# One ordered DMA queue for x and the first weights, more engines summing squares, four residual buffers, fewer layer norm tiles and a shared last norm, in an encoder block on eight cores

## The chip, the cores and the metric

The kernel runs on all 8 cores of one Trainium2 chip, each core on its own 2,048 tokens. The metric is the device time of the slowest core, in microseconds. A program on 8 cores has a fast state and a slow one, in which the cores of a die show a lower granted clock; times of the two states are never compared here. Where one time is given for a kernel it is the median of its runs.

## The reference, cut to what matters

```python
def rms_norm(x, g):
    y = x * rsqrt(mean(x * x, axis=-1) + 1e-6)
    return y * g

# one layer; D = 1024, D_FF = 2816
u = rms_norm(h, g_mix)
z = u @ w_in                                  # value | gate | pool | gate A | gate B
gates = sigmoid(z[..., c3:] + b_gate)
y_conv = silu(layer_norm(depthwise_conv31(a_val * sigmoid(a_gate)))) @ w_conv_out
y_pool = (window_mean_minus_token(p) @ w_pool * pool_scale) @ w_pool_out
h = h + (gates_A * y_conv + gates_B * y_pool) @ w_o
v = rms_norm(h, g_ffn)
h = h + (silu(v @ w_ffn_gate) * (v @ w_ffn_up)) @ w_ffn_down
out = rms_norm(h, g_final)
```

The time goes through these stages in this order: the norm of x and the pool part of `w_in` (the start), value and gate, the convolution, the layer norm (which overlaps with the products of the folded pool weights), `w_o` with the residual, the two FFN projections, the down projection, and the last norm (the tail).

## The kernel before: the parts that the change touches

`tt`, `stt` and `act` issue one elementwise instruction on the engine named; `mm` issues a matmul; `S.dma(E, ...)` starts a transfer from engine E's queue; waits are inserted from what each instruction reads and writes.

The start. x comes in six pieces on SyncE's queue and the weights on GpSimd's queue. GpSimd issues one weight, waits for the first piece to land, and then issues the other eight.

```python
PIECES = ((0, 160), (160, 320), (480, 400), (880, 400), (1280, 400), (1680, 400))

    def x_load(p):
        o, n = PIECES[p]
        S.dma(SP, x_sem[p], xb[p]..., xp_d.ap()[:, KC * o:KC * (o + n)])
    x_load(0)
    # ... three small constants on SP
    for p in range(1, NX):
        x_load(p)
    load_one()
    S.wait_prod(POOL, x_sem[0])
    prefetch()

    def s1_squares(p):
        # ... p == 0: four squares on ACT, four on DVE, and the sums on TensorE
        for h in range(4):
            act(sq[:, 2 * h:2 * h + 2, :], x[:, 2 * h:2 * h + 2, :], AF.Square)
        tt(DVE, sq[:, 0:2, :], sq[:, 0:2, :], sq[:, 2:4, :], ALU.add)
        tt(DVE, sq[:, 4:6, :], sq[:, 4:6, :], sq[:, 6:8, :], ALU.add)
        tt(DVE, sq[:, 0:2, :], sq[:, 0:2, :], sq[:, 4:6, :], ALU.add)
        tt(DVE, sq[:, 0, :], sq[:, 0, :], sq[:, 1, :], ALU.add)

    def s1_norm(p):
        # ... matmul with ones over the squares, Ln and Exp on ACT into psum[7]
        for k in range(KC):
            stt(DVE, uT[:, k, o:o + n], xb[p][:, k, :], pcc(PC_GMIX, k), psum[7][:, 0:n], ALU.mult, ALU.mult)
```

The layer norm normalises each 512-token block in place on VectorE (`ln_steps`):

```python
        for c in range(KC):
            tt(DVE, d, d, mean[:], ALU.subtract)
            tt(DVE, d, d, rstd[:], ALU.mult)
```

The residual stage. The squares for the FFN norm go through three tiles `sq1`, GpSimd adds them up, and the log of the norm is written into `sq1[0]`, one of the three:

```python
            q = sq1[c % 3][:, 0:w_]
            act(q, src, AF.Square)
            tt(eng, a, a, q, ALU.add)             # eng is GpSimd in this stage
    def rms_stat(n, w_=TT):
        mm(psum[6][:, 0:w_], ones[:], ac1[n % 2][:, 0:w_], True, True)
        t = sq1[0][:, 0:w_]
        act(t, psum[6][:, 0:w_], AF.Ln, bias=e_rms)
        act(psum[7][:, 0:w_], t, AF.Exp, scale=-0.5)
```

The tail: the last norm has eight products on VectorE, and each is sent out from SyncE's queue.

```python
        for c in range(KC):
            x = h[:, c, o:o + w_]
            stt(DVE, x, x, pcc(PC_GFIN, c), psum[7][:, 0:w_], ALU.mult, ALU.mult)
            if w_ < TT:
                S.dma(SP, out_sem, out_d.ap()[b][...], x)
```

## Time and profile before

| | us |
|---|---|
| first three runs | 1098.68 median (1076.29 to 1101.15), two of them slow |
| the two fast runs of four | 1076.29 and 1077.07 |
| span of the slowest core in the profile (core 2) | 1074.0 |
| TensorE busy in it | 1008.9 |

Part 1 and part 2 of the page of the kernel before. Part 1 has busy time, share and instruction count of each engine; in part 2 each digit is the busy share, in tenths, of one fortieth of the span (27 us).

```profile
PE 1008.9 (94%) x5642; PEld 492.8 (46%) x5708; DVE 456.3 (42%) x710; ACT 310.1 (29%) x509; POOL 129.0 (12%) x160
PE   3788999999998999999998899999999999999996
PEclk9988999999999999999999899999999999999998
```

TensorE works all the time except for the first 110 us, a few places in the middle and the end. So whatever a change wins comes from the 65 us in which TensorE waits, and from the half-clock matmuls behind those waits. The view of waits of TensorE says for what; its columns are the total in us, how often, and the longest.

```profile
PE ps L353 <- DVE uT L374: 10.1, 13, 2.4
PE ps L353 <- DVE sqx L367: 7.9, 2, 7.4
PE ps L353 <- DMA wslot_61<-w_in: 5.4, 1, 5.4
PE ps L353 <- DMA wslot_62<-w_in: 5.1, 1, 5.1
PE ps L353 <- ACT zt_203 L364: 4.8, 1, 4.8
PE ps L353 <- DMA wslot_63<-w_in: 4.6, 1, 4.6
PE ps L353 <- DVE h1b_219 L367: 4.1, 1, 4.1
```

`uT`, `sqx` and the three weight slots belong to the start, `zt` to the layer norm stage and `h1b` to the residual stage. Why the weights are late shows in the DMA issues of the first 12 us; the last number of a row is the time from issue to landing.

```profile
xb_177<-xp SPq DMA_DIRECT2D x1, 640.0 KB, 5.6
wslot_61<-w_in POOLq DMA_DIRECT2D x1, 256.0 KB, 13.8
wslot_63<-w_in POOLq DMA_DIRECT2D x1, 256.0 KB, 24.9
```

A weight of 256 KB takes 14 to 25 us from issue to landing: it shares the DMA engines, whose busy share is 1.01 from 8 to 41 us, with x pieces of 1,280 and 1,600 KB that were issued before it. These weights are also issued late, at 7.3 us or after, because GpSimd first waits for the first piece. The end of the timeline shows the tail (start, duration, engine, what, and in brackets the idle time before it).

```profile
1065.39 0.43 DVE L367 TENSOR_TENSOR ac_0_223<-ac_0_223,sq_1_221 128x256 f32<-128x256 f32 x1 [0.73 <-ACT sq_1_221 L364]
1067.96 3.22 DVE L374 SCALAR_TENSOR_TENSOR h2b_259<-h2b_259,pc_s,ps 128x256 f32<-128x256 f32 x8 [2.14 <-ACT ps L364]
1068.51 3.82 SPq L190 DMA_DIRECT2D out<-h2b_259  x8
```

Eight products take 3.22 us and their eight issues on one queue 3.82 us; the span ends 1.7 us after the last issue.

### The profile page before, as it was taken

The numbers are of one execution on the slowest core, as the hardware profiler recorded it, in microseconds if no ns is written. First come the engines' busy times: TensorE is split into PE (matmuls) and PEld (weight loads), VectorE is DVE, ScalarE is ACT, GpSimd is POOL, SyncE is SP. The second block draws the span as 40 slices with busy tenths as digits, with TensorE's granted clock in tenths as the row PEclk, the third lists the DMA queues.
The fourth block names the chain that finished last, engine by engine and source line by source line (L and its number), as shares of the span: only waits on it lengthen the run. The fifth ranks groups of instructions, "written<-read, shape, count | busy, mean of one in ns | idle before, by whom it ended". The sixth has DMA issues, their size and how long they took to land.

```text
span 1073.3 us, 15749 instructions; the slowest of 8 cores (1070.5 to 1074.0 us)
## 1 busy us (share of the span) xinstructions
PE 1014.0 (94%) x5708; PEld 493.1 (46%) x5708; DVE 456.2 (43%) x710; ACT 310.1 (29%) x509; POOL 128.7 (12%) x160
## 2 busy tenths in 40 slices
PE   3688999999998999999998999999999999999996
PEld 2444555555443444444443344444444444444485
DVE  2344569995369532332536432122211221243454
ACT  2443333433477822212132421111111111111121
POOL 1000312241011000000063501111000000000000
PEclk9988999999999999999999899999999999999998
DMA  9600796776627011212744935656222100604112
GB/s 253 161 1 1 115 205 139 150 175 152 120 36 113 1 30 30 30 31 30 192 171 157 220 55 94 93 93 91 42 40 40 31 1 29 206 1 157 79 79 79
DMA packets 34379, 99.90 MB, mean 93 GB/s; under 512 B 4096, under 2 KB 7296, under 8 KB 31744
## 3 DMA queue, kind: packets, MB, share of 16 engines
q0 software_dynamic: 17024, 35.13, 21.3%
q1 hardware_dynamic: 17280, 63.77, 20.4%
q8 instruction: 47, 0.77, 0.3%
q14 instruction: 28, 0.23, 0.1%
HBM read 111.93 MB, written 21.04 MB: 124 GB/s over the span
## 4 chain that ended last, share of the span: by engine, by line
PE 83%; DVE 6%; DMA 5%; issue 2%; ACT 1%; POOL 1%; SPq 0%; DVEq 0%; ACTq 0%; POOLq 0%
PE ps L353 79%; PE ps L618 5%; DMA wslot_63<-w_in 2%; DVE vT L374 1%; DMA rep_186<-ad 1%; DMA rep_187<-ad 1%; DMA ad<-aT_183 1%; POOL ac_0_223 L367 1%; POOL ac_1_224 L367 0%; DVE uT L374 0%; DMA xb_177<-xp 0%; ACT ps L364 0%; DVE sqx L367 0%; DVE h2b_259 L374 0%; SPq L190 0%
## 5 line engine op out<-in xcount | busy, mean ns | idle before, releaser
L353 PE MATMUL ps<-mT,weff 128*128 128x512 bf16 x256 | 59.3, 379 | 1.5 <-DVE zt_201 L367 1.5
L353 PE MATMUL ps<-uT,wslot_60 128*128 128x512 bf16 (+4 forms) x224 | 51.1, 357 | 4.5 <-DVE uT L374 4.3
L353 PE MATMUL ps<-uT,wslot_65 128*128 128x512 bf16 (+4 forms) x216 | 47.1, 366 | 0.0
L353 PE MATMUL ps<-uT,wslot_61 128*128 128x416 bf16 (+4 forms) x192 | 40.5, 357 | 4.4 <-DMA wslot_61<-w_in 4.4
L353 PE MATMUL ps<-uT,wslot_62 128*128 128x416 bf16 (+4 forms) x192 | 39.5, 350 | 5.1 <-DMA wslot_62<-w_in 5.1
L353 PE MATMUL ps<-uT,wslot_64 128*128 128x416 bf16 (+4 forms) x192 | 41.5, 363 | 0.9 <-DVE zt_200 L367 0.9
L364 ACT ACTIVATE sgf_225<-ps 128x512 f32<-128x512 f32 x30 | 17.9, 597 | 83.3 <-PE ps L353 83.3
L353 PE MATMUL ps<-vT,wslot_67 128*128 128x512 bf16 x160 | 39.3, 381 | 1.6 <-DVE vT L374 1.4
L353 PEld LDWEIGHTS ps<-mT,weff 128*128 128x128 bf16 x256 | 25.0, 98 | 32.3 <-issue 2.5
L364 ACT ACTIVATE sgf_227<-ps 128x512 f32<-128x512 f32 x29 | 17.3, 597 | 77.4 <-PE ps L353 77.4
L364 ACT ACTIVATE sgf_226<-ps 128x512 f32<-128x512 f32 x29 | 17.3, 597 | 77.0 <-PE ps L353 77.0
L353 PE MATMUL ps<-uT,wslot_63 128*128 128x416 bf16 (+3 forms) x128 | 28.0, 346 | 12.1 <-DMA wslot_63<-w_in 5.8
L353 PE MATMUL ps<-vT,wslot_64 128*128 128x512 bf16 x160 | 38.8, 386 | 0.0
L353 PE MATMUL ps<-vT,wslot_63 128*128 128x512 bf16 x160 | 37.8, 379 | 0.0
L353 PE MATMUL ps<-vT,wslot_66 128*128 128x512 bf16 x160 | 37.8, 379 | 0.0
L353 PE MATMUL ps<-vT,wslot_61 128*128 128x512 bf16 x160 | 37.8, 379 | 0.0
L353 PE MATMUL ps<-vT,wslot_62 128*128 128x512 bf16 x160 | 37.8, 379 | 0.0
L353 PE MATMUL ps<-vT,wslot_68 128*128 128x512 bf16 x160 | 37.8, 379 | 0.0
L353 PE MATMUL ps<-vT,wslot_65 128*128 128x512 bf16 x160 | 37.8, 379 | 0.0
L353 PEld LDWEIGHTS ps<-uT,wslot_60 128*128 128x128 bf16 x224 | 21.9, 98 | 31.6 <-issue 13.2
L353 PEld LDWEIGHTS ps<-uT,wslot_65 128*128 128x128 bf16 x216 | 21.5, 101 | 22.8 <-issue 3.2
L353 PE MATMUL ps<-uT,wslot_68 128*128 128x416 bf16 (+1 forms) x144 | 30.9, 357 | 0.0
(1660 smaller groups left out, 1962.9 us busy)
## 6 DMA issues: line engine op xcount, KB each, us to landing
rep_186<-ad SPq DMA_DIRECT2D x32, 263.0 KB, 6.5
rep_187<-ad SPq DMA_DIRECT2D x32, 263.0 KB, 7.6
h1b_217<-xr SPq DMA_DIRECT2D x2, 2048.0 KB, 11.5
h1d<-h1b_217 SPq DMA_DIRECT2D x2, 2048.0 KB, 7.1
h2b_259<-h1d SPq DMA_DIRECT2D x2, 2048.0 KB, 9.4
h1b_218<-xr SPq DMA_DIRECT2D x1, 2048.0 KB, 18.9
h1b_219<-xr SPq DMA_DIRECT2D x1, 2048.0 KB, 11.0
h1d<-h1b_218 SPq DMA_DIRECT2D x1, 2048.0 KB, 15.6
```

What stands on the lines that cost most here:

```text
L353: S.op(PE, lambda e: e.matmul(out, lhsT=lhsT, rhs=rhs, start=start, stop=stop), [lhsT, rhs], [out], signal=stop if signal is None else signal)
L364: S.op(ACT, lambda e: e.activation(out=out, in_=in_, func=func, scale=scale, **kw), reads, [out])
L367: S.op(eng, lambda e: e.tensor_tensor(out=out, in0=a, in1=b, op=op), [a, b], [out])
L374: S.op(eng, lambda e: e.scalar_tensor_tensor(out=out, in0=a, scalar=s, in1=b, op0=op0, op1=op1), [a, b] + ([] if isinstance(s, float) else ...
L618: S.op(PE, lambda e, o=o, lt=lt, r_=r_, q=q, j=j: e.matmul(o, lhsT=lt, rhs=r_, start=(q == 0), stop=(q == 7), tile_position=(0, 32 * j)), ...
```

## The change

Its intent: let each weight arrive just before the matmuls that need it, take the sums of squares off VectorE at the start, free layer norm tiles, load the fourth residual block early, and share the last norm between two engines and two DMA queues. The diff, cut to its core (left out: renamings; buffer addresses; the scaling of the pool weights, which moves from VectorE to GpSimd; and three scalings by `g_final` that ScalarE does ahead of the three products on GpSimd):

```diff
-PIECES = ((0, 160), (160, 320), (480, 400), (880, 400), (1280, 400), (1680, 400))
+PIECES = ((0, 160), (160, 256), (416, 320), (736, 416), (1152, 448), (1600, 480))
@@ x and weights in one queue; the wait of GpSimd for the first piece goes
-        S.dma(SP, x_sem[p], xb[p]...)
+        S.dma(POOL, x_sem[p], xb[p]...)
-    for p in range(1, NX):
+    for p in range(NX):
         x_load(p)
-    load_one()
-    S.wait_prod(POOL, x_sem[0])
+        if p < 4:
+            load_one()
+            load_one()
     prefetch()
@@ squares: the first three pieces summed on TensorE, the others on GpSimd
-        if p == 0:
+        if p < 3:
-        tt(DVE, sq[:, 0:2, :], sq[:, 0:2, :], sq[:, 2:4, :], ALU.add)    # and three more
+        tt(POOL, sq[:, 0:2, :], sq[:, 0:2, :], sq[:, 2:4, :], ALU.add)   # and three more
@@ a new order of tiles, norms and squares; its end:
+    tiles((3,), range(4))
+    s1_squares(5)
+    s1_norm(4)
+    tiles((3,), range(4, KC))
+    tiles((4,), range(1))
+    s1_norm(5)
+    tiles((4,), range(1, KC))
+    tiles((5,), range(KC))
@@ layer norm: the last block uses no zt tiles; the folded pool weights free two more
-    zorder = list(range(NZT - 3, NZT)) + list(range(2, NZT - 3))
+    zorder = list(range(NZT - 3, NZT)) + list(range(NZT - 3))
@@ residual: four buffers, block 3 loaded at the outset
-    x_res(0)
-    x_res(1)
+    for b in (0, 1, 3):
+        x_res(b)
@@ last norm: three of eight products on GpSimd, their outputs on ScalarE's queue
+        if last:
+            rs = sgf[0][:, 0:w_]
+            act(rs, sq1[0][:, 0:w_], AF.Exp, scale=-0.5)
+        for c in (4, 0, 5, 1, 6, 2, 3, 7) if last else range(KC):
+            side = last and c in (4, 5, 6)
+            if side:
+                tt(POOL, x, x, rs, ALU.mult)
+            else:
+                stt(DVE, x, x, pcc(PC_GFIN, c), psum[7][:, 0:w_], ALU.mult, ALU.mult)
             if w_ < TT:
-                S.dma(SP, out_sem, ...)
+                S.dma(ACT if side else SP, out_sem, ...)
@@ and the last square goes straight into a second matmul with ones instead of an add
```

More of the change, by code (lines that the diff above doesn't have):

```diff
@@ L272, in build_nc @@
     weff = at("weff", [128, KC, 1024], BF16, oW)
-    xoffs = [oM, oM + 160 * 32, oM + 480 * 32, oW, oZ, oZ + 400 * 32]
+    xoffs = [oM, oM + 160 * 32, oM + 416 * 32, oZ, oZ + 416 * 32, oW]
     xb = [at(f"xb{i}", [128, KC, n], F32, o) for i, ((_, n), o) in enumerate(zip(PIECES, xoffs))]
@@ L280, in build_nc @@
     aT = [at(f"aT{i}", [128, EXT], BF16, z + i * EXT * 2) for i in range(2)]
-    wps = at("wps", [128, 4, 2, 256], BF16, z)
     z += 2 * EXT * 2
@@ L300, in build_nc @@
     h1b = [at("h1b0", [128, KC, TT], F32, oM), at("h1b1", [128, KC, TT], F32, oM + 16384),
-           at("h1b2", [128, KC, TT], F32, oZ + 16384)]
+           at("h1b2", [128, KC, TT], F32, oZ + 16384), at("h1b3", [128, KC, TT], F32, oW)]
     sq1 = [at(f"sq1_{i}", [128, TT], F32, oZ + i * 2048) for i in range(3)]
@@ L305, in build_nc @@
     vT = at("vT", [128, KC, TOK], BF16, oA)
-    foff = [oW + i * 4096 for i in range(4)] + [oM + i * 4096 for i in range(8)] + \
+    foff = [oM + i * 4096 for i in range(8)] + [oW + i * 4096 for i in range(4)] + \
            [oB + i * 4096 for i in range(10)]
@@ L344, in build_nc @@
     ad_sem = [dsem(f"d_ad{i}") for i in range(2)]
-    h1_sem = [dsem(f"d_h1{i}") for i in range(3)]
+    h1_sem = [dsem(f"d_h1{i}") for i in range(NB)]
     sp_sem = [dsem(f"d_sp{i}") for i in range(NB)]
@@ L455, in x_load @@
         o, n = PIECES[p]
-        S.dma(SP, x_sem[p], xb[p][:].rearrange("p k t -> p (k t)"), xp_d.ap()[:, KC * o:KC * (o + n)])
-    x_load(0)
+        S.dma(POOL, x_sem[p], xb[p][:].rearrange("p k t -> p (k t)"), xp_d.ap()[:, KC * o:KC * (o + n)])
     for (o, i_) in ((pc[:], pc_d.ap()), (invc[:], ic_d.ap()), (emask[:], em_d.ap())):
         S.dma(SP, cst, o, i_, val=48)
-    for p in range(1, NX):
+    for p in range(NX):
         x_load(p)
-    load_one()
-    S.wait_prod(POOL, x_sem[0])
+        if p < 4:
+            load_one()
+            load_one()
     prefetch()
@@ L484, in s1_squares @@
             act(sq[:, 2 * h:2 * h + 2, :], x[:, 2 * h:2 * h + 2, :], AF.Square)
-        tt(DVE, sq[:, 0:2, :], sq[:, 0:2, :], sq[:, 2:4, :], ALU.add)
-        tt(DVE, sq[:, 4:6, :], sq[:, 4:6, :], sq[:, 6:8, :], ALU.add)
-        tt(DVE, sq[:, 0:2, :], sq[:, 0:2, :], sq[:, 4:6, :], ALU.add)
-        tt(DVE, sq[:, 0, :], sq[:, 0, :], sq[:, 1, :], ALU.add)
+        tt(POOL, sq[:, 0:2, :], sq[:, 0:2, :], sq[:, 2:4, :], ALU.add)
+        tt(POOL, sq[:, 4:6, :], sq[:, 4:6, :], sq[:, 6:8, :], ALU.add)
+        tt(POOL, sq[:, 0:2, :], sq[:, 0:2, :], sq[:, 4:6, :], ALU.add)
+        tt(POOL, sq[:, 0, :], sq[:, 0, :], sq[:, 1, :], ALU.add)
     def s1_norm(p):
@@ L492, in s1_norm @@
         st = psum[6][:, 0:n]
-        ks = (0, 4, 1, 5, 2, 6, 3, 7) if p == 0 else (0,)
+        ks = (0, 4, 1, 5, 2, 6, 3, 7) if p < 3 else (0,)
         for i, k in enumerate(ks):
@@ L509, in pool_tile, with tiles @@
             release(f"pool{c}")
+    def tiles(ps, cs):
+        for c in cs:
+            for p in ps:
+                pool_tile(p, c)
     s1_squares(0)
@@ L513, in build_nc @@
     s1_squares(1)
-    for c in range(4):
-        pool_tile(0, c)
+    tiles((0,), (0, 1))
     s1_norm(1)
+    tiles((1,), (0, 1))
     s1_squares(2)
-    for c in range(4):
-        pool_tile(1, c)
-    for c in range(4, KC):
-        pool_tile(0, c)
-        pool_tile(1, c)
-        if c == 5:
-            s1_norm(2)
-        if c == 6:
-            s1_squares(3)
-    for p in range(2, NX):
-        for c in range(KC):
-            pool_tile(p, c)
-            if c == 2 and p + 1 < NX:
-                s1_norm(p + 1)
-            if c == 5 and p + 2 < NX:
-                s1_squares(p + 2)
+    tiles((0, 1), (2, 3))
+    s1_norm(2)
+    tiles((0, 1), (4, 5))
+    s1_squares(3)
+    tiles((2,), range(6))
+    s1_squares(4)
+    tiles((0, 1, 2), (6,))
+    s1_norm(3)
+    tiles((0, 1, 2), (7,))
+    tiles((3,), range(4))
[6 more added lines that the diff above has]
+    tiles((5,), range(KC))
     win_done = set()
@@ L707, in ln_stat @@
         mm(pq[:], ones[:], acc_q[:, tok], True, True)
-        i = ztile()
-        act(zt[i][:], pm[:], AF.Square)
         if b == NB - 1:
-            mean, rstd = pm, psum[7]
-            ids = (i,)
-        else:
-            m_ = ztile()
-            act(zt[m_][:], pm[:], AF.Copy)
-            mean, rstd = zt[m_], zt[i]
-            ids = (i, m_)
-        tt(DVE, zt[i][:], pq[:], zt[i][:], ALU.subtract)
-        lnm[b] = (mean, rstd, ids)
+            var, mean, rstd = acc_q[:, tok], pm[:], psum[7][:]
+            ids = ()
+        else:
+            ids = (ztile(), ztile())
+            var, mean = zt[ids[0]][:], zt[ids[1]][:]
+            rstd = var
+        act(var, pm[:], AF.Square)
+        if b < NB - 1:
+            act(mean, pm[:], AF.Copy)
+        tt(DVE, var, pq[:], var, ALU.subtract)
+        lnm[b] = (var, mean, rstd, ids)
     def ln_rstd(b):
-        mean, rstd, ids = lnm[b]
-        act(zt[ids[0]][:], zt[ids[0]][:], AF.Ln, bias=e_ln)
-        act(rstd[:], zt[ids[0]][:], AF.Exp, scale=-0.5)
+        var, _, rstd, _ = lnm[b]
+        act(var, var, AF.Ln, bias=e_ln)
+        act(rstd, var, AF.Exp, scale=-0.5)
     def ln_steps(b):
-        mean, rstd, ids = lnm[b]
+        _, mean, rstd, ids = lnm[b]
         out = []
@@ L731, in step @@
                 d = d_sb[c][b][:]
-                tt(DVE, d, d, mean[:], ALU.subtract)
-                tt(DVE, d, d, rstd[:], ALU.mult)
+                tt(DVE, d, d, mean, ALU.subtract)
+                tt(DVE, d, d, rstd, ALU.mult)
             out.append(step)
@@ L743, in silu, with wps @@
             act(actT[c][b][:], d_sb[c][b][:], AF.Silu, bias=pcc(PC_LNB, c), scale=pcc(PC_LNG, c))
+    def wps(g, km):
+        return slot[whome[f"wpl{g}"]][:, km * 512:km * 512 + 256]
     def wps_scale(g):
-        s_ = whome[f"wpl{g}"]
         for km in range(2):
-            src = slotf[s_][:, km * 256:(km + 1) * 256]
-            ts(DVE, wps[:, g, km, :], src, pcc(PC_PSC, 2 * g + km), ALU.mult)
+            src = slotf[whome[f"wpl{g}"]][:, km * 256:(km + 1) * 256]
+            ts(POOL, wps(g, km), src, pcc(PC_PSC, 2 * g + km), ALU.mult)
     def fold(g):
@@ L756, in fold @@
                 for km in range(2):
-                    mm(ps[:], wps[:, g, km, ki * 128:(ki + 1) * 128],
+                    mm(ps[:], wps(g, km)[:, ki * 128:(ki + 1) * 128],
                        w(f"po{2 * g + km}", None, h * 512, (h + 1) * 512), km == 0, km == 1)
@@ L793, in build_nc @@
     fold(3)
-    zfree.extend((0, 1))
     for c in range(2):
@@ L816, in x_res @@
     def x_res(b):
-        q = b % 3
-        S.dma(SP, h1_sem[q], h1b[q][:].rearrange("p k t -> p (k t)"), xr_d.ap()[b])
-    x_res(0)
-    x_res(1)
+        S.dma(SP, h1_sem[b], h1b[b][:].rearrange("p k t -> p (k t)"), xr_d.ap()[b])
+    for b in (0, 1, 3):
+        x_res(b)
     for b in range(NB):
@@ L835, in sumsq, with rms_stat @@
             tt(eng, a, a, q, ALU.add)
-    def rms_stat(n, w_=TT):
-        mm(psum[6][:, 0:w_], ones[:], ac1[n % 2][:, 0:w_], True, True)
+    def rms_stat(n, w_=TT, last=None):
+        mm(psum[6][:, 0:w_], ones[:], ac1[n % 2][:, 0:w_], True, last is None)
+        if last is not None:
+            mm(psum[6][:, 0:w_], ones[:], last, False, True)
         t = sq1[0][:, 0:w_]
@@ L843, in v_norm @@
     def v_norm(b):
-        h = h1b[b % 3]
+        h = h1b[b]
         for c in range(KC):
@@ L854, in build_nc @@
                 mm(ps[:], w(f"wo{c}", k), mrg[k][b][:], k == 0, k == KC - 1)
-            h = h1b[b % 3][:, c, :]
+            h = h1b[b][:, c, :]
             tt(DVE, h, ps[:], h, ALU.add)
@@ L862, in build_nc @@
                 v_norm(b - 1)
-                if b == 1:
-                    x_res(3)
     def gu(j, b):
@@ L903, in build_nc, with out_norm @@
         h2_load(b)
-    def out_norm(b, o, w_, n, eng):
+    def out_norm(b, o, w_, n, last=False):
         h = h2b[b % 3]
-        for c in range(KC):
+        if last:
+            rs = sgf[0][:, 0:w_]
+            act(rs, sq1[0][:, 0:w_], AF.Exp, scale=-0.5)
+        for c in (4, 0, 5, 1, 6, 2, 3, 7) if last else range(KC):
             x = h[:, c, o:o + w_]
-            stt(DVE, x, x, pcc(PC_GFIN, c), psum[7][:, 0:w_], ALU.mult, ALU.mult)
+            side = last and c in (4, 5, 6)
[3 more added lines that the diff above has]
+                stt(DVE, x, x, pcc(PC_GFIN, c), psum[7][:, 0:w_], ALU.mult, ALU.mult)
             if w_ < TT:
-                S.dma(SP, out_sem, out_d.ap()[b][:, c * TT + o:c * TT + o + w_], x)
+                S.dma(ACT if side else SP, out_sem, out_d.ap()[b][:, c * TT + o:c * TT + o + w_], x)
         if w_ == TT:
@@ L922, in build_nc @@
             tt(DVE, x, ps[:, 0:w_], x, ALU.add)
-            sumsq(x, n, c, DVE, w_)
+            if n == 4 and c == KC - 1:
+                act(sq1[c % 3][:, 0:w_], x, AF.Square)
+            else:
+                sumsq(x, n, c, DVE, w_)
+            if n == 4 and c in (4, 5, 6):
+                act(x, x, AF.Identity, scale=pcc(PC_GFIN, c))
             if c == 1 and n > 0:
@@ L926, in build_nc @@
                 rms_stat(n - 1, pw_)
-                out_norm(pb, po, pw_, n - 1, DVE)
+                out_norm(pb, po, pw_, n - 1)
                 if n == 1:
                     h2_load(3)
-    rms_stat(4, 256)
-    out_norm(3, 256, 256, 4, DVE)
+    rms_stat(4, 256, sq1[(KC - 1) % 3][:, 0:256])
+    out_norm(3, 256, 256, 4, True)
     S.wait_prod(SP, out_sem)
```

## The prediction

> **What bounds the kernel now.** TensorE: the page's first part shows it busy 1008.9 of 1074.0 us, so about 65 us of waits can go. The busy table by stretches puts them at 0 to 41 us (25 us), 51 to 97 us (8), 260 to 400 us (11), 585 to 610 us (9) and after 1064 us (9).
>
> **1. Start.** In the timeline x piece 0 lands at 6.7 us, but the second to fourth pool weights only at 21.1, 27.5 and 33.3 us: both queues share the DMA engines (share 1.01 from 8 to 41 us). TensorE waits 5.4 + 5.1 + 4.6 us for weights, then twice about 2.4 us for squares and norm (59 and 90 us), each followed by half-clock matmuls (400 columns in 0.36 us, not 0.17). Half rate after idling is in the Trainium skill, TensorE: Matmul & The Clock Gate, Part 1; the trace agrees. The first value/gate matmul starts at 115.5 us; at full clock the pool tiles need about 56 us.
>
> With one ordered queue each weight comes just before its tiles; total DMA work is unchanged (about 40 us). I walked the new order through with trace durations. The change adds 14 float32 square matmuls (about 6 us of TensorE) and GpSimd adds: at 1.27 us per 512 columns about 7 to 8.4 us a piece, against 3.66 us on VectorE (the Trainium skill, GPSIMD Engine Reference, section 3, says about twice as slow; the trace has 1.27 against 0.69 us). Data stop limiting after about 15 us; the chain square, sum, norm, uT (VectorE, 0.55 us per 400-column slice) limits then. I get value/gate starting near 96 us (88 to 104): gain **19 us**.
>
> **2. Layer norm tiles.** The 4.8 us wait for a gate tile (333 us), with 1.7 us of half clock behind it, is lack of a free tile; the change removes it. But VectorE is the chain there (44 us of norm steps from 309 us), so TensorE then waits for PSUM that VectorE has not drained. Gain **3 us**, not 8.
>
> **3. Four residual buffers.** The fourth x load (issued 571, landed 582 us) was used only at 590 us. The 4.1 us wait at 586 us is VectorE behind the FFN norm, whose log waits for GpSimd's adds (1.41 us apart) to free a square tile. The change leaves that chain. Gain **0**.
>
> **4. Last norm.** One add less (0.6 us), five VectorE products and DMA issues on one queue instead of eight (0.48 us each). Gain **1.7 us**.
>
> **Sum.** 24 us from 1076 us: **1053 us** in the fast state, 2.2% faster. Two of three runs before were in the slow state (about 1100 us), which I then expect near 1076 us. Range **1036 to 1078 us**. Chances: faster by over 2% 0.55, within 2% 0.42, slower 0.03.
>
> **What would show it.** 1: waits for pool weights gone, value/gate starting at 88 to 104 us, waits for uT and GpSimd's square sums instead. 2: the 4.8 us wait gone, longer waits for VectorE's zt products near 350 us. 3: the wait for h1b late in the residual stage still about 4 us. 4: last matmul to end 8 us, not 10.
>
> **What would make it wrong.** If the software queue moves x slower than the 290 GB/s now seen, or GpSimd's adds slow VectorE, the start gains under 10 us. If TensorE keeps full clock through the VectorE-paced tiles and norms overlap better than I walked, up to 28 us. If the residual stage's chain restarts earlier for another reason, 4 to 6 us more.

## The result, and the profile after

The kernel after took 1068.18 us (1066.94 to 1068.62, four runs, all fast); the kernel before, in the same rounds, 1087.88 us over four runs, of which two were fast (1076.29 and 1077.07). The ratio is 0.9919, with a 95% interval from 0.9895 to 0.9943: 8.7 us, where 24 us were predicted. A ratio here is the mean time of one kernel's fast runs over that of the other's of the same rounds, so it is not quite the ratio of the medians quoted.

To see where the gain came from, I took a few moments from the trace of each core and their median over the eight cores, in us from the start of the span.

| | before | after | difference |
|---|---|---|---|
| first x piece landed | 6.5 | 9.3 | +2.8 |
| first value/gate matmul (end of the start) | 114.3 | 102.0 | -12.3 |
| from there to the last convolution matmul | 177.3 | 177.0 | -0.3 |
| to the first product of the folded pool weights | 42.6 | 37.5 | -5.1 |
| to the last of those products | 182.8 | 186.5 | +3.7 |
| residual stage: first `w_o` product to first FFN matmul | 64.8 | 64.8 | 0.0 |
| first FFN matmul to last down-projection matmul | 466.4 | 466.6 | +0.2 |
| tail: from there to the end | 9.9 | 15.0 | +5.1 |

The stages sum to the result: -12.3, -1.4 for the layer norm, 0 and +5.1 make -8.6.

Part 1 of the page after, and the same rows of part 2:

```profile
PE 1012.4 (95%) x5738; PEld 497.1 (47%) x5738; DVE 438.8 (41%) x686; ACT 309.7 (29%) x513; POOL 164.5 (15%) x189
PE   4989999999998999999998899999999999999994
PEclk9989999999999999999999999999999999999998
```

The start is denser; the last slice has gone from 6 to 4 tenths. TensorE's waits after:

```profile
PE ps L352 <- DVE sqx L366: 10.9, 1, 10.9
PE ps L352 <- DVE uT L373: 7.5, 17, 1.8
PE ps L352 <- DVE h1b_218 L366: 4.1, 1, 4.1
PE ps L352 <- ACT zt_206 L363: 1.8, 1, 1.8
PE ps L352 <- DVE zt_197 L366: 1.5, 1, 1.5
PE ps L352 <- DVE zt_211 L366: 1.5, 1, 1.5
```

The three waits for weights are gone. The wait for the very first squares (`sqx`) has grown from 7.4 to 10.9 us. The 4.8 us wait for a `zt` tile has become several of about 1.5 us, most of them on VectorE. The 4.1 us wait for `h1b` is still there. The DMA issues of the first 12 us say why the first squares are late:

```profile
xb_177<-xp POOLq DMA_DIRECT2D x1, 640.0 KB, 8.6
wslot_61<-w_in POOLq DMA_DIRECT2D x1, 256.0 KB, 10.2
wslot_63<-w_in POOLq DMA_DIRECT2D x1, 256.0 KB, 15.0
```

The weights land much earlier, but the first piece of x takes 8.6 us on GpSimd's queue, where it took 5.6 us on SyncE's (these are the slowest cores; over the eight cores the medians are 7.8 and 5.4 us). It is also issued 0.5 us later, at 1.6 us instead of 1.1. Now the tail: the timeline of core 3, the slowest, then the last two stretches of its busy table (busy us and count per engine, granted clock, DMA share, GB/s), then the end of its chain of waits (start, us, engine).

```profile
1053.34 2.05 DVE L373 SCALAR_TENSOR_TENSOR h2b_259<-h2b_259,pc_s,ps 128x256 f32<-128x256 f32 x5 [2.48 <-ACT ps L363]
1053.72 2.09 POOL L366 TENSOR_TENSOR h2b_259<-h2b_259,sgf_225 128x256 f32<-128x256 f32 x3 [214.69 <-ACT sgf_225 L363]
1053.89 2.31 SPq L190 DMA_DIRECT2D out<-h2b_259  x5
1054.52 1.71 ACTq L190 DMA_DIRECT2D out<-h2b_259  x3
```

```profile
1055.00:1060.00 5.00, 0.00 (x0) 0.00 (x0) 0.39 (x1) 0.00 (x0) 0.81 (x2) 0.59 0.55 191
1060.00:1066.00 6.00, 0.00 (x0) 0.00 (x0) 0.00 (x0) 0.00 (x0) 0.00 (x0) 0.50 0.00 0
```

```profile
1053.72 0.72 POOL h2b_259 L366
1054.44 0.68 POOLq L955
1055.12 0.68 POOL h2b_259 L366
```

The norm itself went as planned: five products and three, issued by 1056.2. But the span ends at 1065.4, and in its last 5 us no engine is busy and no byte moves. The chain ends with a GpSimd product at 1055.8 us. What lies behind it is not a counted instruction. The raw records of the trace have it (start, end, sequencer, instruction; the records of core 3, most left out):

```
1055.09  1055.81  POOL   third product of the last norm
1058.15           (last output landed)
1053.76  1065.12  POOLq  DRAIN
1058.23  1058.23  SPq    DRAIN
1065.25  1065.27  POOLq  releases the closing barrier of the program
1065.30  1065.35  PEldq  leaves the barrier: end of the span
```

GpSimd's closing drain stands in its queue from 1053.76 and ends 9.3 us after GpSimd's last product, 7 us after the last output has landed, and all engines wait for it. On all eight cores it is the same 9.3 us. In the kernel before GpSimd had nothing to do after about 850 us, so its drain (852.3 to 857.3 us on core 2) lay under other work. There it ended 4.5 us after GpSimd's last instruction, the issue of a weight.

### The profile page after: what moved, and what is told of

The parts are those of the page before. It is cut to its first block, busy times and chain, and to the rows that moved or that the text cites. A ratio compares the mean times of both kernels' runs of the same rounds, so it can differ in the third digit from the quotient of the medians.

```text
span 1065.4 us, 15822 instructions; the slowest of 8 cores (1060.9 to 1065.4 us)
## 1 busy us (share of the span) xinstructions
PE 1012.4 (95%) x5738; PEld 497.1 (47%) x5738; DVE 438.8 (41%) x686; ACT 309.7 (29%) x513; POOL 164.5 (15%) x189
## 4 chain that ended last, share of the span: by engine, by line
PE 83%; DVE 7%; issue 3%; ACT 2%; POOL 2%; DMA 2%; SPq 0%; DVEq 0%; POOLq 0%; ACTq 0%
PE ps L352 79%; PE ps L625 5%; DVE uT L373 1%; DVE vT L373 1%; DMA rep_186<-ad 1%; POOL ac_1_224 L366 1%; POOL ac_0_223 L366 1%; DMA xb_177<-xp 1%; ACT ps L363 1%; ACT sqx L363 0%; ACT sq_1_221 L363 0%; ACT sq_0_220 L363 0%; ACT L363 0%; SPq L190 0%; DVEq L184 0%
## 5 line engine op out<-in xcount | busy, mean ns | idle before, releaser
L352 PE MATMUL ps<-uT,wslot_60 128*128 128x512 bf16 (+6 forms) x224 | 52.8, 354 | 10.5 <-DVE uT L373 7.5
L352 PE MATMUL ps<-uT,wslot_65 128*128 128x512 bf16 (+6 forms) x216 | 45.4, 357 | 0.0
L352 PE MATMUL ps<-uT,wslot_61 128*128 128x416 bf16 (+6 forms) x192 | 41.8, 365 | 0.0
L352 PE MATMUL ps<-uT,wslot_64 128*128 128x416 bf16 (+6 forms) x192 | 38.8, 346 | 1.3 <-DVE zt_210 L366 1.3
L352 PE MATMUL ps<-uT,wslot_62 128*128 128x416 bf16 (+6 forms) x192 | 39.3, 350 | 0.0
```

The source lines that it names most:

```text
L352: S.op(PE, lambda e: e.matmul(out, lhsT=lhsT, rhs=rhs, start=start, stop=stop), [lhsT, rhs], [out], signal=stop if signal is None else signal)
```

## The experiments

The first theory, called G in the quoted expectations, is that the tail is lost to GpSimd's closing drain, which now starts late. The main rival, Q, is that the outputs from ScalarE's DMA queue land late; any further letter is another rival, whose forecast stands in the text. For the start, the question is which part of it gave the gain and where the other 7 us of the predicted 19 went. Kernels whose name starts with a are the kernel after with one thing changed, those with b or d the kernel before with one thing changed. Stages and "drain" (from the end of GpSimd's last instruction to the end of its drain) are medians over the cores of the profiled execution. Every kernel passed the comparison with the reference.

### The tail

**a_tdve**: the last three products on VectorE, outputs still on ScalarE's queue.

```diff
-                tt(POOL, x, x, rs, ALU.mult)      # rs and its Exp go too
+                tt(DVE, x, x, psum[7][:, 0:w_], ALU.mult)
```

> After, with the three shared products of the last norm given back to VectorE (they stay on ScalarE's DMA queue). Theory G (GpSimd had work near the end, and its drain at the end of the program, 11.4 us long in the trace of after, now ends the program although all output had landed 7 us earlier): from the last down-projection matmul to the end about 8.5 us instead of 15.0, ratio to before about 0.986 (6 to 7 us below after). Rival Q (the second hardware DMA queue, ScalarE's, is what is slow to close): 15 us stays, ratio 0.992. Rival P (the prediction: sharing saves 1.7 us): giving the products back costs 0.5 to 1 us, ratio 0.993.

Measured: 1059.81 to 1061.94 us in the three fast runs (one slow run at 1203.76), ratio to before 0.9862 [0.9843, 0.9880]. From the last matmul to the end it is 8.4 us instead of 15.0. The drain still takes 9.3 us, but it begins long before the end and is hidden. G holds; Q falls, since ScalarE's queue is still in use.

**a_tsp**: all outputs on SyncE's queue, the products as in after.

```diff
-                S.dma(ACT if side else SP, out_sem, ...)
+                S.dma(SP, out_sem, ...)
```

> After, with all eight last output DMAs issued by SyncE and the three products left on GpSimd. Theory G: no change, 15 us from the last down-projection matmul to the end, ratio 0.992. Rival Q (ScalarE's DMA queue is slow to close): falls to about 9 us, ratio 0.987.

Measured: 1067.21 us, ratio 0.9920 [0.9905, 0.9936]; the tail 15.0 us, drain 9.3. The last output lands 1.7 us later than in after and the end doesn't move. Q falls a second time.

**b_pool8**: the kernel before with one tiny GpSimd add ahead of the last norm.

```diff
     rms_stat(4, 256)
+    tt(POOL, sgf[0][:, 0:8], sq1[0][:, 0:8], sq1[0][:, 0:8], ALU.add)
     out_norm(3, 256, 256, 4, DVE)
```

> Before, plus one GpSimd add of 128x8 that reads the last log, so it runs about 3.5 us after the last matmul; nothing reads its result. Theory G: GpSimd's drain ends about 9.3 us after that add whatever its size, so the program ends about 13 us after the last down-projection matmul instead of 9.9: 3 us slower, ratio 1.003. If the drain grows with the amount of GpSimd work (rival): under 1 us, ratio 1.000.

Measured: 1076.00 us, ratio 1.0003 [0.9985, 1.0021]; drain only 3.0 us, hidden under the tail of 10.0. This missed what I expected: a late GpSimd instruction alone doesn't make the long drain. Something else in the change lengthens it.

**b_tail**: the shared last norm alone, on the kernel before (the last two pieces of the diff above).

```diff
+            side = last and c in (4, 5, 6)
+            if side:
+                tt(POOL, x, x, rs, ALU.mult)
... and the rest of the shared norm, as in the change
```

> Before with the last norm's change alone (squares in the matmul, three products on GpSimd, two DMA queues), the start as before. GpSimd's drain took 3.0 us after its last instruction in before's start and 9.3 us in the new start. If the long drain belongs to the new start, the shared last norm alone gains about what was predicted: last down-projection matmul to end about 8.7 us instead of 9.9, ratio 0.999. If GpSimd's three 128x256 products make the drain long by themselves: 15.0 us, ratio 1.005.

Measured: 1075.54 us, ratio 0.9991 [0.9973, 1.0009]; tail 9.0 us against 9.9, drain 3.0. So the shared norm by itself gains about 0.9 us by the stages of the trace; in the times alone the gain is within the noise. It is a loss only together with another part of the change. Even the short drain takes part of the gain: the last output lands 8.2 us after the last matmul, and the drain ends at 8.8.

### The start

**b_start**: the start of the change alone on the kernel before (pieces, queue, squares, order).

```diff
-        S.dma(SP, x_sem[p], xb[p]...)
+        S.dma(POOL, x_sem[p], xb[p]...)
... with the new PIECES, order and GpSimd sums, as in the change
```

> Before with the start alone changed (one queue, new pieces and order, squares on TensorE and GpSimd). If the parts add: first value/gate matmul at 102 to 103 us instead of 114 to 115, 12.5 us gained, ratio 0.9885, last matmul to end unchanged at 9.9 us. That is more than after as a whole gains (0.9919), if the tail gave the difference back. The prediction put this part at 19 us: ratio 0.982.

Measured: 1063.96 us, ratio 0.9890 [0.9874, 0.9905]. The first value/gate matmul starts at 101.8 us. Its drain is 9.3 us but hidden, and its tail 9.9 us. One part of the change gains more than the whole. The layer norm stage of this kernel has the old sums, 43.0 and 182.8 us, so the two differences in that stage come from the layer norm part of the change: the fewer tiles, or the scaling of the pool weights that left VectorE with them (eight instructions of 0.35 us just before the norm steps). No run separates these two.

**a_x0sp**: the first x piece back on SyncE's queue.

```diff
-        S.dma(POOL, x_sem[p], xb[p]...)
+        S.dma(SP if p == 0 else POOL, x_sem[p], xb[p]...)
```

> After, with x piece 0 alone sent back to SyncE's hardware queue, first in it; pieces 1 to 5 and the weights stay in GpSimd's queue. If the missing part of the start is the late landing of piece 0 (9.3 us, median of the cores, against 6.5 before): it lands near 6.5 us and the first value/gate matmul moves from 102.0 to about 99 us, ratio 0.989. If the later chain (square, sum, norm, uT) sets the end of the stage by itself: under 1 us.

Measured: 1064.85 us, ratio 0.9897 [0.9882, 0.9911]. The piece lands at 6.3 us instead of 9.3 and value/gate starts at 99.7 us, 2.3 us earlier than in after. Most of the late landing of the first piece is on the critical path.

**a_swap**: the norm of piece 4 ahead of the squares of piece 5.

```diff
     tiles((3,), range(4))
-    s1_squares(5)
     s1_norm(4)
+    s1_squares(5)
     tiles((3,), range(4, KC))
-    tiles((4,), range(1))
+    tiles((4,), range(4))
     s1_norm(5)
-    tiles((4,), range(1, KC))
+    tiles((4,), range(4, KC))
```

The fourth tile instead of the first before the norm of piece 5 is part of the edit too. It was built for what the timeline of the kernel after shows on ScalarE and VectorE between 66 and 76 us:

```profile
66.52 3.67 ACT L363 ACTIVATE sqx<-xb_182 128x960 f32<-128x960 f32 x4
70.09 0.59 ACT L363 ACTIVATE ps<-ps,eps_s 128x448 f32<-128x448 f32 x1
71.47 4.82 DVE L373 SCALAR_TENSOR_TENSOR uT<-xb_181,pc_s,ps 128x448 bf16<-128x448 f32 x8 [11.28 <-ACT ps L363]
```

The statistics of piece 4 are ready at 66.8 us, but its log waits 3.3 us behind the squares of piece 5; VectorE stands idle for 11 us, and TensorE is then paced by the `uT` slices. The matmuls of 448 columns after that take 0.28 us, and 2 us later 0.21 (eight in 2.22 and in 1.68 us); the granted clock in the busy table is 0.50 from 76.9 to 78.6 us, 0.73 over the first of these groups and 1.00 after it. Half rate after idling is what the Trainium skill has in "TensorE: Matmul & The Clock Gate", Part 1; here the trace shows a granted clock of 0.50, and half mixed with full rate over this group of eight.

> After, with the norm of piece 4 put before the squares of piece 5 in program order, and the norm of piece 5 after the fourth tile of piece 4. In after ScalarE does the squares of piece 5 (3.7 us) before the log of piece 4, so uT of piece 4 comes late, TensorE is paced by it for 4 us and drops to half clock. If that is what the start lacks: first value/gate matmul 4 us earlier (98 us), ratio 0.988. If GpSimd's adds (8.1 us for piece 5) limit: under 1 us, or later.

Measured: 1061.80 and 1061.91 us in the two fast runs (two slow ones at 1091 and 1251), ratio 0.9866 [0.9846, 0.9886]. Value/gate starts at 97.7 us, 4.3 us earlier.

**a_dveadd**: the sums of squares back on VectorE, in the new order.

```diff
-        tt(POOL, sq[:, 0:2, :], sq[:, 0:2, :], sq[:, 2:4, :], ALU.add)   # all four adds
+        tt(DVE, sq[:, 0:2, :], sq[:, 0:2, :], sq[:, 2:4, :], ALU.add)
```

> After, with the sums of squares of pieces 3 to 5 on VectorE again instead of GpSimd. Prediction's reading (GpSimd's slow adds limit the start): first value/gate matmul 3 to 5 us earlier. Reading from the trace of after (the adds are done before TensorE asks for them): within 1 us of 102. For GpSimd's drain at the end (9.3 us after its last instruction in all kernels with the new start, 3.0 us in before with one small add): if the float32 adds of the start make it long, 3 us, and 8.5 to 9.5 us from last matmul to end; if the x loads on GpSimd's queue do, 9.3 us and 15.0 us.

Measured: only one of five runs was fast, 1071.04 us, so there is no ratio. In its profile value/gate starts at 105.5 us, 3.5 us later than in after. So GpSimd's slow sums (7.2 to 8.1 us a piece) seem to help: with them TensorE waits 7.5 us for `uT`, without them 9.3, which fits with VectorE having 3.8 to 4.3 us of adds a piece less ahead of `uT`. Drain still 9.3 us: those sums aren't what lengthens it.

**a_xsp**: all x pieces back on SyncE's queue, the rest as in after. GpSimd issues its weights at once, without the old wait for the first piece.

```diff
-        S.dma(POOL, x_sem[p], xb[p]...)
+        S.dma(SP, x_sem[p], xb[p]...)
```

> After, with all six x loads on SyncE's queue (the weights, in the same order, stay alone in GpSimd's), everything else as in after. If the x loads on GpSimd's queue make its drain long: drain 3.0 us, last matmul to end about 9 us instead of 15.0. If the burst of instructions or something else of the new start does: 9.3 and 15.0. For the start: if the single ordered queue is what brings its gain, the pool weights come late again and the first value/gate matmul goes back to 108 us or later; if the new pieces and order do, it stays within 2 us of 102.

Measured: 1062.74 us, ratio 0.9859 [0.9844, 0.9875]. Value/gate starts at 103.8 us, only 1.8 us later than with the single queue, while the tail falls to 8.7 us with a drain of 3.0. In this kernel the single ordered queue is worth 1.8 us at the start and costs 6.3 us at the end. One reason shows in the landings (medians of the cores): the second to fourth weights land at 12.2, 16.8 and 22.6 us here, 12.5, 17.4 and 18.7 in after, and 20.3, 26.5 and 32.8 in before. So they are early with x on SyncE's queue as well; there too GpSimd no longer waits for the first piece before it issues them.

### What lengthens the drain

**d_x5pool**: before, with the tiny add and the last x piece on GpSimd's queue. **d_xall**: the same with all six pieces there, in the old order of issue (all x first, and GpSimd still waits for the first piece).

```diff
-        S.dma(SP, x_sem[p], xb[p]...)
+        S.dma(POOL if p == 5 else SP, x_sem[p], xb[p]...)      # d_x5pool
+        S.dma(POOL, x_sem[p], xb[p]...)                         # d_xall
```

> Before with the 128x8 GpSimd add near the end (as in b_pool8) and one of the six x loads, piece 5, issued from GpSimd's queue (first in it, so the start is disturbed; only the drain is read). If x loads on that queue make the drain long: 9.3 us after the add instead of 3.0, or a sixth of the way (about 4 us) if each load adds its share. If only the whole burst of 15 DMAs does it, or something else of the new start: 3.0 us.

> Before with the 128x8 GpSimd add near the end and all six x loads on GpSimd's queue, in before's pieces and order (the start is disturbed; only the drain is read). If the loads together make it long: 9.3 us after the add, so the program ends about 16 us after the last down-projection matmul. Else 3.0 us and 10.

Measured: drain 3.0 us in both (1078.3 us, and 1085.59 us with value/gate as late as 122.1 us, because the weights then land behind all of x). x loads on that queue are not enough.

**a_oldpieces**: after, with the piece sizes of before. **a_wait1**: after, with GpSimd waiting for piece 1 before it issues piece 3, so that fewer transfers are outstanding.

```diff
-PIECES = ((0, 160), (160, 256), (416, 320), (736, 416), (1152, 448), (1600, 480))
+PIECES = ((0, 160), (160, 320), (480, 400), (880, 400), (1280, 400), (1680, 400))     # a_oldpieces
@@
     for p in range(NX):
+        if p == 3:
+            S.wait_prod(POOL, x_sem[1])                                                # a_wait1
         x_load(p)
```

> The kernel after with the piece sizes of the kernel before (160, 320, four of 400 columns), everything else as after: x on GpSimd's queue between the weights, the new order of compute. One look, for the length of GpSimd's closing drain and the end. If the drain is long because of the larger x pieces (up to 480 columns, rows of 15,360 bytes against 12,800), it is 3.0 us here and the end is about 9 us after the last down-projection product. If it is long because x and weights alternate in the one queue, it stays 9.3 us and the end 15 us. The start should be within 4 us of after either way.

> The kernel after, but GpSimd waits for x piece 1 to land before it issues piece 3, so that fewer transfers wait in its queue at once; order and sizes as after. If the number of outstanding transfers makes the long drain, it is 3.0 us here and the end 9 us after the last product; if the order or the sizes do, it stays 9.3 us and 15 us. I expect that it stays 9.3, because an earlier run with 14 outstanding gave 3.0.

Measured: drain 9.3 us in both (the fast runs took 1076.09 and 1069.62 us). Neither the larger pieces nor the number of outstanding transfers makes it. The first also missed its forecast for the start: value/gate at 110.0 us, 8 us later than in after, not within 4. With these sizes the new order of tiles fits badly; the waits for `uT` rise from 7.5 to 11.2 us.

**d_alt**: d_xall, but x and weights issued alternately as in the change. Old sizes, old order of compute, old last norm.

```diff
-    for p in range(1, NX):
-        x_load(p)
-    load_one()
-    S.wait_prod(POOL, x_sem[0])
+    for p in range(NX):
+        x_load(p)
+        if p < 4:
+            load_one()
+            load_one()
```

> The kernel before, with the 128x8 GpSimd add ahead of the last norm and with x and the first weights issued alternately in GpSimd's queue exactly as in the change; piece sizes, compute order and last norm as before. It differs from the earlier look with all six x loads on that queue (drain 3.0 us) only in the order of issue, and in GpSimd no longer waiting for the first piece. If the alternating order in the queue makes the long drain, it is 9.3 us here; if the new order of compute is needed as well, it is 3.0 us. I expect 9.3. The end stays about 10 us after the last down-projection product either way, because the drain starts ahead of the last norm.

Measured: the drain is 9.3 us, from a GpSimd add of only 8 columns. So what GpSimd issues at the start, and no part of the new compute, sets the length, and by all the runs it is the order: the drain is 3.0 us in the five experiments in which x and weights do not alternate there (b_pool8, b_tail, d_x5pool, d_xall, a_xsp), and 9.3 us in after and in the thirteen in which they do. (d_alt also drops GpSimd's wait for the first piece. But a_xsp drops it too and has 3.0 us, and a_wait1 puts a wait back and has 9.3. All of x first without that wait was not run.) The tail was 13.2 us, not the 10 that I expected, since the drain ends after the outputs. In this one look two cores of one die ran at a lower clock, so its time, 1090 us, says nothing; the other six cores spanned 1060 to 1066 us.

It also showed something about the start: with nothing of the new compute order, value/gate starts at 102.3 us, 12.0 us earlier than in before. So the alternating queue is worth as much as the whole new start, and a_xsp shows that the new order without it is worth 10.5 us; these gains don't add. But both kernels also drop GpSimd's wait for the first piece, and the landings given with a_xsp make it likely that this brought the weights there 8 to 10 us earlier. It may be what both gains share; no run drops only the wait.

### The layer norm and the residual stage

**a_lnt**: the log of the FFN norm in a tile of its own instead of `sq1[0]`.

```diff
+    lnt = at("lnt", [128, TT], F32, oZ + 38912)
-        t = sq1[0][:, 0:w_]
+        t = lnt[:, 0:w_]
-            act(rs, sq1[0][:, 0:w_], AF.Exp, scale=-0.5)
+            act(rs, lnt[:, 0:w_], AF.Exp, scale=-0.5)
```

> After, with the log of the FFN norm written to a tile of its own instead of a square tile that GpSimd's add must first free. The prediction named this as the cause of the 4.1 us wait at the end of the residual stage: then the log comes about 3.6 us earlier, the wait goes, and the residual stage (first product with w_o to first FFN matmul) takes 60 to 61 us instead of 64.8; ratio 0.988. If ScalarE's squares themselves are late behind VectorE: unchanged, 0.992.

Measured: 1060.53 us, ratio 0.9849 [0.9829, 0.9868]. The residual stage takes 58.0 us instead of 64.8, and the 4.1 us wait for `h1b` is gone from TensorE's waits. A further 2.9 us came between the first FFN matmul and the last of the down projection (463.7 against 466.6 us), which no run here explains; its cores lie between 462.7 and 467.3 us, and best1, which has the same edit, takes 465.1. The 6.8 us confirm the cause that the prediction gave in its third point, and show the gain that four buffers could not reach.

**a_lnpool**: the mean of blocks 1 and 2 subtracted on GpSimd. **a_lnskip**: those subtractions left out, wrong (it passed the comparison all the same, presumably because the mean over 1,024 channels is small for these inputs).

```diff
-                tt(DVE, d, d, mean, ALU.subtract)
+                tt(POOL if b in (1, 2) else DVE, d, d, mean, ALU.subtract)   # a_lnpool
+                if b not in (1, 2):                                          # a_lnskip
+                    tt(DVE, d, d, mean, ALU.subtract)
                 tt(DVE, d, d, rstd, ALU.mult)
```

> After, with the mean subtraction of the layer norm for token blocks 1 and 2 (16 of the 64 VectorE steps, 11 us) on GpSimd. If VectorE is what the stage waits for once the tile wait is gone (TensorE waits 5.8 us for zt products there): from the last convolution to the end of the products with the folded pool weights 3 to 5 us less than the 224.0 us of after, ratio 0.988. If VectorE is not the limit: no gain; if GpSimd's slower adds and its place in the weight prefetch become the limit: longer.

> After, without the mean subtraction for token blocks 1 and 2 (a wrong result on purpose: 16 of 64 VectorE steps, 11 us, gone, no wait taken away). If VectorE is what TensorE waits for in this stage: the 5.8 us of waits for zt products go, and the stretch from the last convolution to the last product with the folded pool weights falls by 4 to 6 us (from 224.0 to about 219). If VectorE is not the limit: unchanged.

TensorE's waits of the two, a_lnpool first. (The program's buffer numbers are missing in these runs.)

```profile
PE ps L352 <- DVE zt L366: 12.4, 5, 6.5
```

```profile
PE ps L352 <- DMA wslot<-w_pool_out: 3.8, 1, 3.8
PE ps L352 <- ACT zt L363: 2.4, 2, 1.8
```

a_lnpool took 1076.95 us, ratio 1.0001 [0.9985, 1.0017]: the span of the pool products grew from 186.5 to 194.8 us, because GpSimd's subtractions, 1.45 us each, stand inside the chain. It missed and says nothing about VectorE. a_lnskip took 1063.69 us, ratio 0.9882 [0.9855, 0.9909]; the two parts of the layer norm stage fell from 224.0 to 219.2 us together, and TensorE no longer waits for VectorE's `zt`, only for a weight and for ScalarE. VectorE is the limit in that part after the change, as the prediction said.

### Together

**best1**: a_tdve, a_x0sp, a_swap and a_lnt in one kernel (their four edits as shown).

```diff
... the edits of a_tdve, a_x0sp, a_swap and a_lnt
```

> After with four corrections together: piece 0 of x on SyncE's queue, the norm of piece 4 before the squares of piece 5, the FFN norm's log in its own tile, and the last products on VectorE. From the single runs: 2.3 + 4.3 + 6.8 + 6.6 us, about 20 us below after if they add: 1048 us, ratio 0.973. If the start's two corrections overlap: 1050 us.

Measured: 1046.87 us (1044.20 to 1048.49, four fast runs), ratio 0.9719 [0.9701, 0.9737], and the fast runs of the kernel before took 1075.48 to 1077.26. It beats both kernels. Part 1 of its page and its longest waits at the start:

```profile
PE 1010.3 (97%) x5738; PEld 498.1 (48%) x5738; DVE 440.2 (42%) x689; ACT 309.3 (30%) x512; POOL 162.7 (16%) x185
PE ps L353 <- DVE uT L374: 7.6, 12, 2.8
PE ps L353 <- DVE sqx L367: 6.4, 1, 6.4
```

Value/gate starts at 95.5 us, the residual stage is 58.0 us, the tail 8.3 us.

## Why the prediction was right or wrong

The predicted time, 1053 us, was 15 us too low, although 1068 lies in the range. The gain was 8.7 us and not 24. Term by term:

**Step 4, the last norm: predicted "Gain 1.7 us", measured a loss of 5.1. This step failed in sign.** Its sum of saved instructions was right: the last output lands 7.8 us after the last matmul, where it was 9.6 in before, 1.7 us sooner. What it left out is that this program ends only when every engine has drained, that GpSimd's work had not been near the end before, and that its drain takes 9.3 us in this kernel. The span then ends 7 us after the last output. The prediction gave "last matmul to end 8 us, not 10" as the sign of being right, and it was 15.0. Two parts of the change make this loss only together: the alternating queue lengthens the drain (d_alt), and the shared norm puts it at the end (a_tdve, b_start). Nor was the third engine needed: with all eight products on VectorE (a_tdve) the last output lands at 8.0 us and the tail is 8.4, shorter than with GpSimd's three and the short drain (8.7 in a_xsp, 9.0 in b_tail).

**Step 1, the start: predicted 19 us, measured 12.3. The mechanism was right and the size was off.** The waits for weights went, and waits for `uT` took over, as it said. Value/gate started at 102.0 us, inside the 88 to 104 given, not at 96. The missing 6 us are found: the first piece lands 2.8 us later on GpSimd's queue, and putting it back gains 2.3 us (a_x0sp); on ScalarE the squares of the last piece stand ahead of a log that is due, and swapping them gains 4.3 us (a_swap). With both, best1 starts value/gate at 95.5 us. So the prediction's walk through the new order missed these two delays; that a slower queue for x could cost part of the gain stood among its risks. The worry that GpSimd's sums might hurt was wrong the other way (a_dveadd: 3.5 us worse without them, in its one fast run).

**Step 2, the layer norm tiles: predicted 3 us, measured 1.4.** The 4.8 us wait goes, the stage starts 5.1 us sooner, and 3.7 us come back as waits for VectorE. That giving back was in the prediction, which put the net at 3 us instead of 8; the step's mechanism held and its size was off, since the net was 5.1 less 3.7. That VectorE limits is shown by a_lnskip; how much of the 5.1 us is owed to the freed tiles and how much to the scaling moved off VectorE is not shown.

**Step 3, four residual buffers: predicted 0, measured 0.0.** The cause named was right too: freeing the square tile takes 6.8 us off this stage (a_lnt).

The sum of the misses, 6.8 us at the tail, 6.7 at the start and 1.6 in the layer norm, is the 15 us between the forecast and the result.

What stays open: why the order of issue on GpSimd's queue changes its closing drain from 3.0 to 9.3 us, since the records show only its length; how much of the start's gain is owed to dropping GpSimd's wait for the first piece; the part of the scaling in the layer norm's gain; and the 2.9 us that a_lnt gains after its own stage.

## What to carry to other kernels

Before you move work to another engine near the end of a program, look at when that engine finished until now and how long its closing drain is: work that is cheap in busy time can put a drain of several us at the end of the span. When a change mixes several parts, run its parts alone; here one part was better than the whole, and two parts of the start, each worth over 10 us, did not add. A tile that is shared between two uses for convenience is worth checking before buffers are added: one extra tile for a log took 6.8 us off a stage in which a whole residual buffer gained nothing.

## What the Trainium skill lacked or had wrong

- "VectorE: DVE Perf Modes", section "The DRAIN you can't avoid", has drains of about 12 ns on all five engines, from the preamble and postamble that the runtime puts around a program. The drains here stand at the kernel's own lines. The opening ones agree on four engines (7 to 10 ns on core 3 of after), but GpSimd's takes 0.17 us, and GpSimd's closing drain ends 3.0 or 9.3 us after GpSimd's last instruction in the experiments (within 0.03 us on all cores of a run) and 4.4 to 4.7 us after it in before. No page says that this drain is long, that it changes with the order in which x and weights were issued (d_xall 3.0, d_alt 9.3), or that late work on GpSimd can so add 6.6 us to a program (a_tdve).
- "DMA: Bandwidth & Descriptors", section "Issuing engines are not separate DMA queues", says that issuing from several engines saves only the issue time on the sequencer, usually small. Here, with the first piece of x sent from SyncE instead of GpSimd (a_x0sp), the issue came 0.5 us sooner and the piece landed 3.0 us sooner: its 640 KB took 5.2 us from issue to landing instead of 7.8 (medians of the cores), and 2.3 us were on the critical path. The first-byte latencies on that page, about 1 and 0.6 us in its Specifications, differ by 0.4 us, not by these 2.6.
- "GPSIMD Engine Reference", section 3, has GpSimd about twice as slow as VectorE elementwise. The trace agrees (1.27 against 0.69 us for 512 columns). What no page has is a number for moving such work there all the same where VectorE is the limit: here the start was 3.5 us faster with the sums on GpSimd (a_dveadd, one fast run).
